# A new written order for the opening of a hybrid decoder step, with the state loads placed behind the gate's bias

## The chip, the cores and the metric

The kernel runs on one core of one Trainium2 chip. The metric is the device time of one execution in microseconds, lower is better; the kernel before took 1208.33 us, the median of three runs. The engines are TensorE (PE, matrix products; PEld is its weight load), VectorE (DVE), ScalarE (ACT), GpSimd (POOL) and SyncE (SP), which here only issues transfers. Each engine works through its own list of instructions in order and waits where an operand isn't ready.

## The reference

One layer of a hybrid decoder is computed for a prompt of 1024 rows and for 64 sample rows (8 sequences of 8), with model width 1024:

```python
mod = silu(c) @ w_ada + b_ada
shift, scale, gate = split(mod, 3)
h = rmsnorm(x, norm_g) * (1 + scale) + shift
u_pool, z_pool, z_ssm, xbc, dt_raw, g_raw = split(h @ w_in, SPLITS)
p = (pool_mix(u_pool, pool_buf) * silu(z_pool)) @ w_pool_out
xbc_c = silu(causal_conv(xbc, conv_buf, conv_w, conv_b))
y = SSD(xbc_c, softplus(dt_raw + dt_bias), -exp(a_log), ssm_state) + d_skip * xs
s = gated_rmsnorm(y, silu(z_ssm)) @ w_ssm_out
x = x + gate * ((sigmoid(g_pool) * p + sigmoid(g_ssm) * s) @ w_o)
```

`pool_buf` and `conv_buf` (the last rows of the pooling branch and of the convolution) and `ssm_state` are states that the sample rows bring along; new ones are returned beside the final rmsnorm of `x`.

## The kernel before

Everything is held transposed, 128 channels on the partitions and the 1088 rows (1024 of the prompt, 64 of the samples) along the free axis, in three blocks of 256, 384 and 448 rows (`BLK`). A product in full precision is made of three in a shorter format: each operand is cut into a high half (a copy in that format) and a low half (the rest, a subtraction), and high times high, low times high and high times low are summed.

The program has two parts. The **opening** (`first`, L604 on) reads `x`, normalizes and transposes it, forms the modulation from `w_ada`, makes `h` with both halves, and computes the first columns of `h @ w_in`: two of the gate's columns directly (L817), then a pair of columns by seven half-sized products (L958), `dt` (L843) and the `gate` vector (L870). Behind it the column pairs go on through `product` (L412), and then the rest of the layer. The order in the later part is found by a planner; the order of the opening is written by hand: the string `ORDER1` is a list of words, each word calls one short function that emits the instructions of one step, and `in_line` ties the instructions of each engine to each other in the order in which they were emitted. So the place of a word sets where its instructions stand on each engine that it uses. A letter behind a word names the engine: `.V` is DVE, `.G` POOL, `.A` ACT.

The words that this text speaks of (`b` a block, `k` one of eight slices of 128 channels):

- `warmN`: N matmuls whose result nobody reads. `sq`, `root`, `unit`, `spread`, `rsb`: the norm of the rows, spread over the partitions. `turn`b.k and `out`b.k: the transposed tile on PE, and its product with the norm on DVE (L703) into the tile `tf`.
- `ada`p.k: part p of silu(c) @ w_ada on PE (L736). `mr`, `end`, `md`: its copy, its transposition (L744) and the scale and shift, `md0` to `md3` for two slices each (L751, L754).
- `h`b.k: high half of `h` on ACT (L767, L769). `t`, `ta`: the same value in full in `tf` (L776 on ACT, L778 on DVE; for sample columns L785 and L786). `l`b.k: its low half (L644).
- `hi`, `lo`: halves of the first gate-column weights. `pr`b.k: six matmuls of block b with slice k (L817). `sg`: sigmoid and store.
- `ca`, `cb`, `cc`, `ce`: sums and differences of the halves of `tf` (L644, 544 columns) for the seven products; `s1h` to `s4h` and `s1l` to `s4l` their halves; `wh`, `wl` halves of the weight sums; `tc`, `tb`, `d21`, `d12` the weight sums. `m`i.s: twelve matmuls (L958). `u`i.s: their sums.
- `dU`, `dL`, `dR`: the matmuls of `dt` (L843), which read `tf` after the `c` words. `gt`, `ge`: the gate's matmuls (L870), and its sum with the bias on DVE followed by its store to `gate_d`.

`loads` runs after each word and issues, in the order of the list `waiting`, each transfer whose conditions have been said; they go to SP's queue. PSUM banks are handed out in the order of the words. Behind the opening `u_unit` and `conv_unit` begin with loads of the states into small tiles of four buffers; these loads are not part of the written order, and the planner sets them where it finds a place on SP. `tc.issue_after(i)` keeps an instruction behind instruction i on its engine's list.

Of the kernel before, what the change touches and what calls it, by code (L numbers as in the profile page):

```python
# [8 lines left out]
F32 = mybir.dt.float32  # L9
# [37 lines left out]
def tile_pool_ssd_step(  # L47
# [473 lines left out]
    yp_ = [None] * 4  # L521

    def u_unit(gi):
        L = gi + 1
        stp = sm.tile([P, 120], F32, tag="stc", name=nm("stp"), bufs=4)
        load(stp, state_pool[gi])
        pwt = sm.tile([P, P], F32, tag="stc", name=nm("pwt"), bufs=4)
        load(pwt, pool_w[0, gi])
# [66 lines left out]
    def gate_load(k):  # L595
# [21 lines left out]
        ta2.6.A wl4.V pr1.6 l1.7.V sgt t2.6 t2.7 m1.0 cb1.V sg0.0 cc1.V sg0.1 pr1.7 ce1.V h2.7 s1l0.V h2.6
        pr2.5 sg1.1 l2.7.V sg1.0 m1.1 l2.6.V d12.V s4h1 ca2.V pr2.6 wh5 cb2.V s1h2 ca3.V pr2.7 s1l2.V
        s1h3 cb3.V cc2.V gt0 wh3 u1.0 sg2.0 wl3.G u1.1 dR0 wh2 gt2 sg2.1 ce2.V dR1 cc3.V s2h0 gt4 wl2.V
        s4h2 dU1 ce3.V s2h3 s4l2.V s2h2 dL0 dUo1 s2l3.V dU0 s4h3 s2l0.V z1.0 s2l2.V gt6 dUo0 s1l3.V s2h1 dL1  # L620
        ge s4l1.G s3h0 dLo0 m2.0 s3h1 dLo1 s3h3 s3l1.V s3h2 s2l1.V m2.1 u2.0 dsL s3l3.V z1.1 s3l2.V m3.0
# [1668 lines left out]
```

## Time and profile before

| | before |
|---|---|
| median of 3 runs | 1208.33 us (1208.1 to 1209.11) |
| the profiled execution's own time | 1206.63 us |
| its span, first to last instruction | 1204.9 us |
| granted TensorE clock in the span | 0.998 |
| busy: PE, DVE, ACT, POOL | 99%, 76%, 55%, 68% |
| first L412 matmul, the end of the opening on PE | 90.43 us |

Times in the rows are microseconds from the start of the span, unless marked ns. In an order of time, a row is its start, its length, the engine, the line, the operation, the tiles it writes and reads, and a count where neighbours were merged; what stands in brackets is the idle time of the engine ahead of it and what ended it. Matmuls overlap, so that their starts tell more than their lengths.

### The profile page before, as it was taken

What the parts mean: (1) busy time and instruction counts of PE and PEld (TensorE: products, weight loads), DVE (VectorE), ACT (ScalarE), POOL (GpSimd) and SP (SyncE); (2) the same over time, 40 slices, a digit from 0 to 9 for tenths busy, and PEclk for the clock granted to TensorE, in tenths of its full rate; (3) what the DMA queues carried; (4) which work ended last, traced back from release to release, by engine and by line L of the source; (5) the groups of instructions that cost most, each with busy time, mean ns of one, the idle gap of its engine ahead of it and who ended that gap; (6) DMA issues with size and microseconds to landing.
All of it is one profiled execution on the core that took longest, in us unless ns stands there. A gap on an engine that the chain in (4) does not pass through costs nothing.

```text
span 1204.9 us, 25116 instructions
## 1 busy us (share of the span) xinstructions
PE 1190.0 (99%) x9274; PEld 1125.3 (93%) x9274; DVE 915.8 (76%) x1567; ACT 661.4 (55%) x1511; POOL 815.0 (68%) x687
## 2 busy tenths in 40 slices
PE   9999999999999999999999999999999999999997
PEld 8879999999999999999999999999999989999885
DVE  6993689975979587877576564687888988679976
ACT  6864356475665556554534334566686766412435
POOL 1127878877988787755677776376889889523653
PEclk9999999999999999999999999999999999999999
DMA  9836445565546555454576767988788788595794
GB/s 352 305 133 208 141 137 180 185 212 149 185 157 201 172 160 164 149 166 137 191 241 239 239 220 252 322 311 267 238 273 297 263 293 282 204 337 157 236 208 158
DMA packets 156082, 262.69 MB, mean 218 GB/s; under 512 B 31280, under 2 KB 79160, under 8 KB 155960
## 3 DMA queue, kind: packets, MB, share of 16 engines
q1 hardware_dynamic: 87208, 171.25, 42.7%
q10 hardware_dynamic: 64592, 81.91, 19.7%
q0 software_dynamic: 4160, 7.94, 3.1%
q8 instruction: 73, 1.20, 0.4%
q14 instruction: 49, 0.40, 0.1%
HBM read 173.31 MB, written 87.73 MB: 217 GB/s over the span
## 4 chain that ended last, share of the span: by engine, by line
PE 82%; DVE 5%; DMA 4%; POOL 3%; ACT 3%; issue 2%; SPq 0%; DVEq 0%; POOLq 0%; ACTq 0%
PE mm L412 24%; PE ps L412 24%; PE mm L227 15%; PE pc L412 5%; PE ps L1246 2%; PE ps L1249 2%; DMA Y<-in_w_ada 1%; PE ps L2043 1%; PE ps L2042 1%; PE ps L2041 1%; DVE tf L644 1%; PE ps L1513 1%; PE ps L958 1%; PE pc L1335 1%; DMA G<-in_w_ada 1%
## 5 line engine op out<-in xcount | busy, mean ns | idle before, releaser
L227 PE MATMUL mm<-Y,w 128*128 128x352 f32 (+1 forms) x1440 | 255.4, 331 | 0.8 <-DVE G L1976 0.6
L227 PEld LDWEIGHTS mm<-Y,w 128*128 128x128 f32 x1440 | 235.3, 188 | 7.6 <-issue 4.6
L154 POOL TENSOR_TENSOR w<-rawA,w 128x512 fp32r<-128x512 f32 x120 | 181.7, 1518 | 78.6 <-ACT w L151 72.2
L154 POOL TENSOR_TENSOR w<-raw,w 128x512 fp32r<-128x512 f32 x90 | 157.2, 1753 | 62.9 <-ACT w L151 62.7
L412 PE MATMUL mm<-Y,w 128*128 128x272 f32 x1200 | 168.7, 289 | 0.0
L412 PE MATMUL ps<-Y,w 128*128 128x272 f32 x1200 | 167.8, 289 | 0.0
L412 PEld LDWEIGHTS mm<-Y,w 128*128 128x128 f32 x1200 | 156.8, 188 | 2.6 <-issue 1.0
L412 PEld LDWEIGHTS ps<-Y,w 128*128 128x128 f32 x1200 | 157.1, 188 | 0.8 <-issue 0.6
L151 ACT ACTIVATE w<-rawA 128x512 fp32r<-128x512 f32 x120 | 75.2, 626 | 95.1 <-PE ps L412 53.8
L1090 DVE SCALAR_TENSOR_TENSOR GA<-GA,cvT,GA 128x1112 f32<-128x1112 f32 x72 | 126.1, 1756 | 0.1
L151 ACT ACTIVATE w<-raw 128x512 fp32r<-128x512 f32 x90 | 56.0, 628 | 102.7 <-PE ps L412 33.7
L412 PE MATMUL mm<-G,w 128*128 128x272 f32 x720 | 101.2, 289 | 0.0
L412 PE MATMUL ps<-G,w 128*128 128x272 f32 x720 | 100.6, 289 | 0.0
L412 PEld LDWEIGHTS mm<-G,w 128*128 128x128 f32 x720 | 94.1, 188 | 1.2 <-issue 0.9
L412 PEld LDWEIGHTS ps<-G,w 128*128 128x128 f32 x720 | 94.4, 188 | 0.3 <-issue 0.3
L1234 ACT ACTIVATE dec<-dec,acT 128x128 f32<-128x128 f32 x256 | 78.6, 390 | 18.7 <-POOL dec L1230 18.6
L291 POOL TENSOR_TENSOR pw<-pw 128x512 fp32r<-128x512 f32 x40 | 65.6, 1639 | 11.5 <-ACT pw L290 11.5
L412 PE MATMUL pc<-Y,w 128*128 128x272 f32 x480 | 67.2, 288 | 0.0
L412 PEld LDWEIGHTS pc<-Y,w 128*128 128x128 f32 x480 | 62.6, 188 | 0.5 <-issue 0.4
L1470 POOL TENSOR_TENSOR Y<-xb,Y 128x512 fp32r<-128x512 f32 x32 | 41.5, 1296 | 25.0 <-ACT Y L1468 24.8
L1246 PE MATMUL ps<-dec,xd 128*64 128x128 f32 (+1 forms) x576 | 52.3, 273 | 0.6 <-DVE dec L1535 0.5
L1527 POOL TENSOR_TENSOR xl<-xw,xh 128x512 fp32r<-128x512 f32 x32 | 42.5, 1327 | 14.6 <-ACT xh L1526 14.6
(542 smaller groups left out, 2712.0 us busy)
## 6 DMA issues: line engine op xcount, KB each, us to landing
rawA<-in_w_in SPq DMA_DIRECT2D x62, 512.0 KB
ws<-pw ACTq DMA_DIRECT2D x32, 512.0 KB
dec<-acs_d SPq DMA_DIRECT2D x32, 512.0 KB
w<-ws SPq DMA_DIRECT2D x32, 512.0 KB
xbc<-GA ACTq DMA_DIRECT2D x24, 512.0 KB
wo<-ph SPq DMA_DIRECT2D x20, 512.0 KB
Y<-wo SPq DMA_DIRECT2D x10, 1024.0 KB
pw<-in_w_ssm_out ACTq DMA_DIRECT2D x32, 256.0 KB
```

The lines of the kernel that those rows point to most:

```text
L151: ins = act(hi[:, :, :ncols], raw[:, :, :ncols], AF.Copy)
L154: (eng or nc.gpsimd).tensor_tensor(lo[:, :, :ncols], raw[:, :, :ncols], hi[:, :, :ncols].bitcast(F32), ALU.subtract)
L227: mm(ps[:, :n], w[k // 4][h][:, k % 4, :], r[k][:, o:o + n], start=(j == 0), stop=(j == len(terms) - 1))
L291: nc.gpsimd.tensor_tensor(raw.bitcast(F32R), raw, hi.bitcast(F32), ALU.subtract)
L412: mm(p, w[j // 8][:, k], A(k, s)[j // 4 == 1], start=(j == 0), stop=(j == 11))
L644: eng[e].tensor_tensor(dst, x, y, op)
L1090: V.scalar_tensor_tensor(d[:, :n], rp[:, k:k + n], cvT[:, 24 * k + mc:24 * k + mc + 1], d[:, :n], ALU.mult, ALU.add)
L1234: act(dec[:, h], dec[:, h], AF.Exp, bias=acT[:, c, 8 * g + h:8 * g + h + 1], scale=-1.0)
L1246: mm(o[hh], xd[:S, 2 * q + hh, :], dec[:S, 2 * q + hh], start=True, stop=state is None)
L1249: mm(o[hh], state[:, h * 64:h * 64 + 64], cE[:, h], start=False, stop=True)
L1470: nc.gpsimd.tensor_tensor(yl[g][:, :, o:o + S], v, yhc.bitcast(F32), ALU.subtract)
L1527: nc.gpsimd.tensor_tensor(xl, xw, xh.bitcast(F32), ALU.subtract)
```

## The change

`ORDER1` is written anew: nearly the same words in another order, 350 before and 349 now. The `warm` matmuls ahead of the first `turn` grow from 20 to 25, and those behind it shrink from 18 to 11. These words change engine: `lo0.0`, `l2.1`, `l1.3`, `l2.4`, `l1.4`, `wl3` and `s4l1` from POOL to DVE, `l0.5` from DVE to POOL, `ta2.1` and `t0.3` from ACT to DVE, `t0.2` and `t0.4` from DVE to ACT, `unit1` from DVE to ACT. The loads change: `vecs` goes behind the fifth tile of `x`, the first of the two first weight pieces ahead of the sample rows, the second behind part 0 of `w_ada`. The state loads of the first `u_unit` and `conv_unit` go behind the last load of the gate's bias. One tile of the sigmoid has a tag of its own (`g3`).

```diff
     def u_unit(gi):
         L = gi + 1
         stp = sm.tile([P, 120], F32, tag="stc", name=nm("stp"), bufs=4)
-        load(stp, state_pool[gi])
         pwt = sm.tile([P, P], F32, tag="stc", name=nm("pwt"), bufs=4)
-        load(pwt, pool_w[0, gi])
+        with tc.issue_after(calm[0]):
+            load(stp, state_pool[gi])
+            load(pwt, pool_w[0, gi])
...
     ORDER1 = """
-        warm20 sq0.A silu sq1.V turn0.3 turn0.5 turn0.2 tab vt sq2.V turn0.6 turn0.1 root0
...
+        warm20 sq0.A silu sq1.V warm5 turn0.0 turn0.2 turn0.3 warm2 sq2.V tab root0 sq3.A sq4.A
...
-                buf = pa.tile([P, HF], F32, tag=("u3", "u2", "c2", "u3")[2 * b + t], name=nm("g0"))
+                buf = pa.tile([P, HF], F32, tag=("u3", "u2", "c2", "g3")[2 * b + t], name=nm("g0"))
...
-                load(bg[32 * j:32 * j + NB + 1], b_ada[0, 2 * D + 256 * j:2 * D + 256 * j + 256].partition_broadcast(NB + 1))
+                ins = load(bg[32 * j:32 * j + NB + 1], b_ada[0, 2 * D + 256 * j:2 * D + 256 * j + 256].partition_broadcast(NB + 1))
+            calm.append(ins.ins)
...
-        for what in ("x01", "vb", "x27", "smp", "p0", "w", "p1", "p2"):
+        for what in ("x01", "x24", "vb", "x57", "w0", "smp", "p0", "w1", "p1", "p2"):
...
     def conv_unit(mc, g, row):
         stc = sm.tile([P, 24], F32, tag="stc", name=nm("stc"), bufs=4)
-        load(stc, state_conv[mc])
+        with tc.issue_after(calm[0]):
+            load(stc, state_conv[mc])
```

Behind the opening the lists of all engines are the same as before but for a few neighbours. Three places in the opening, as the built programs have them. The first is POOL from the end of its settings (`bg`) to the first weight half of the later part (L154). Before:

```order
L999 MEMSET bg 128x256
L644 TENSOR_TENSOR w_489<-raw_243,w_489 128x512
L644 TENSOR_TENSOR Y_520<-tf_310,Y_519 128x448
L644 TENSOR_TENSOR Y_520<-tf_290,Y_519 128x384
L644 TENSOR_TENSOR G_761<-tf_315,G_760 128x448
L644 TENSOR_TENSOR G_761<-tf_315,G_760 128x384
L644 TENSOR_TENSOR w_1057<-raw_931,w_1057 128x512
L644 TENSOR_TENSOR Y_520<-tf_294,Y_519 128x544
L644 TENSOR_TENSOR w_1213<-rawA_715,w_1213 128x512
L154 TENSOR_TENSOR w_1254<-rawA_1250,w_1254 128x512
```

Now:

```order
L1004 MEMSET bg 128x256
L649 TENSOR_TENSOR G_747<-tf_363,G_746 128x256
L649 TENSOR_TENSOR w_1207<-rawA_709,w_1207 128x512
L154 TENSOR_TENSOR w_1249<-rawA_1245,w_1249 128x512
L154 TENSOR_TENSOR w_1305<-rawA_1245,w_1305 128x512
```

Of eight low halves on POOL one is left (`wl6`, the last ahead of L154), and `l0.5` is new.

The second is DVE from the first product of the sample block (`out2.k`, 128x448; `raw`, `w` are `lo0.0`) to `md0` (the rows that write `md`). Before:

```order
L703 TENSOR_TENSOR tf_298<-ps_405,rsb 128x448
L703 TENSOR_TENSOR tf_366<-ps_423,rsb 128x448
L703 TENSOR_TENSOR tf_310<-ps_435,rsb 128x448
L703 TENSOR_TENSOR tf_315<-mm_412,rsb 128x448
L703 TENSOR_TENSOR tf_290<-ps_483,rsb 128x448
L751 TENSOR_TENSOR md<-ps_491,vT 128x18
```

Now:

```order
L708 TENSOR_TENSOR tf_345<-ps_436,rsb 128x448
L708 TENSOR_TENSOR tf_363<-ps_423,rsb 128x448
L708 TENSOR_TENSOR tf_345<-mm_414,rsb 128x384
L708 TENSOR_TENSOR tf_299<-ps_441,rsb 128x448
L708 TENSOR_TENSOR tf_349<-mm_400,rsb 128x384
L649 TENSOR_TENSOR w_446<-raw_237,w_446 128x512
L708 TENSOR_TENSOR tf_295<-ps_395,rsb 128x448
L756 TENSOR_TENSOR md<-ps_497,vT 128x18
```

Seven instructions stand there now where five stood.

The third is DVE at the last of the `c` words (`tf<-tf,tf`, 128x544; the `c` tile is `u1`, the `w` row `wl2`, `Y`, `S` and `R` low halves of sums), whose results the `dt` matmuls read. Before:

```order
L976 TENSOR_TENSOR c_125_1059<-s_110_900,ps_964 128x272
L976 TENSOR_TENSOR c_125_1059<-s_110_900,mm_1008 128x272
L644 TENSOR_TENSOR tf_306<-tf_306,tf_298 128x544
L644 TENSOR_TENSOR tf_290<-tf_366,tf_290 128x544
L644 TENSOR_TENSOR w_1071<-rawA_633,w_1071 128x512
L644 TENSOR_TENSOR tf_366<-tf_366,tf_290 128x544
L644 TENSOR_TENSOR Y_520<-tf_306,Y_519 128x544
```

Now:

```order
L649 TENSOR_TENSOR tf_349<-tf_349,tf_299 128x544
L649 TENSOR_TENSOR tf_303<-tf_358,tf_303 128x544
L981 TENSOR_TENSOR c_127_1086<-s_109_895,ps_994 128x272
L649 TENSOR_TENSOR tf_358<-tf_358,tf_303 128x544
L981 TENSOR_TENSOR c_127_1086<-s_109_895,ps_962 128x272
L649 TENSOR_TENSOR Y_1082<-tf_295,Y_1082 128x544
L649 TENSOR_TENSOR Y_1082<-tf_303,Y_1082 128x544
L649 TENSOR_TENSOR Y_1082<-tf_299,Y_1082 128x544
L649 TENSOR_TENSOR w_1063<-rawA_622,w_1063 128x512
```

The weight half and one of the two `u1` sums have moved behind the last `c` word (`tf_366` before, `tf_358` now).

More of the change, by code (lines that the diff above doesn't have):

```diff
@@ L617, in tile_pool_ssd_step @@
[L617 to L621, printed above, removed]
@@ L624, in tile_pool_ssd_step @@
+        s2l0.V s2h2 dL0 z1.0 s2h1 s2l3.V s2l2.V dL1 dUo1 wh3 wl2.V dUo0 s1l3.V s4l2.V
+        gt6 s3h0 wl3.V dLo1 s3h3 s4h3 m2.1 s3h1 dLo0 s2l1.V m2.0 s3l0.V s3h2 ge
+        z1.1 s3l1.V u2.0 m3.0 wh6 wl6.G s3l2.V u2.1 s3l3.V m3.1 dRo1 dRo0 u3.1 u3.0
+        s1l1.V m4.0 nw m4.1 dsR s4l1.V wl5.V u4.0 s4l0.V s4l3.V m5.0 nt3 m5.1 dsL
+        u5.0 u4.1 n1 nt2 m6.0 u5.1 n2 u6.0 z5.0 m6.1 z5.1 nd u6.1
     """.split()
@@ L1020, in first @@
                 waiting += [((), lambda: load(xr[8][0][:NS], x_sample.rearrange("b t d -> (b t) d")))]
[L1021 to L1022 removed]
+            elif what[0] == "w":
+                waiting += [((), lambda t=int(what[1]): w_load(t, 0))]
             elif what[0] == "x":
```

38 lines of the change are left out of this document (20 added, 18 removed).

## The prediction

> **What bounds the kernel now.** I read the busy time by stretches first, then TensorE's order of time in the opening, then VectorE's and GpSimd's. In the stretches the columns are the busy time of each engine with its instructions in brackets, the granted clock, the DMA share and GB/s.
>
> ```profile
> 92.00:300.00 208.00, 208.00 (x1643) 206.62 (x1643) 147.71 (x236) 112.01 (x256) 164.72 (x109) 1.00 0.54 173
> 300.00:600.00 300.00, 300.00 (x2374) 295.59 (x2373) 231.00 (x360) 170.82 (x384) 228.51 (x152) 1.00 0.53 170
> 600.00:900.00 300.00, 299.69 (x2440) 279.27 (x2441) 208.16 (x389) 165.25 (x398) 213.17 (x196) 1.00 0.76 259
> ```
>
> From 92 to 900 us TensorE (PE, the first busy figure) is without a gap: 807.69 of 808 us. The change touches nothing there, so what it gains or loses by the first L412 matmul should arrive at the end nearly whole. The question is when that matmul starts. PE's order of time in the opening (start, length, then the instruction, its count, and in brackets the idle time ahead):
>
> ```profile
> 29.65 0.28 PE L817 MATMUL ps<-Y,w 128*128 128x256 f32 x1
> ...
> 34.55 0.33 PE L817 MATMUL ps<-Y,w 128*128 128x384 f32 x1
> ...
> 35.41 0.34 PE L817 MATMUL mm<-Y,w 128*128 128x384 f32 x1
> 35.68 1.95 PE L736 MATMUL pc<-G,scT 128*32 128x128 f32 x64
> ...
> 39.48 0.28 PE L817 MATMUL mm<-Y,w 128*128 128x256 f32 x1
> ...
> 40.43 0.28 PE L817 MATMUL mm<-Y,w 128*128 128x256 f32 x1
> ...
> 41.80 1.96 PE L736 MATMUL pc<-G,scT 128*32 128x128 f32 x64
> ...
> 47.46 0.39 PE L817 MATMUL mm<-G,w 128*128 128x256 f32 x1 [0.18 <-DVE G L644]
> ...
> 52.58 1.78 PE L958 MATMUL ps<-Y,w 128*128 128x272 f32 x12 [0.30 <-ACT s L974]
> 54.20 0.28 PE L817 MATMUL mm<-G,w 128*128 128x256 f32 x1
> ...
> 60.38 0.36 PE L817 MATMUL ps<-G,w 128*128 128x448 f32 x1
> ...
> 61.38 0.36 PE L817 MATMUL mm<-G,w 128*128 128x448 f32 x1
> ...
> 65.60 1.07 PE L870 MATMUL pc<-Y,scT 128*32 128x256 f32 x16
> ...
> 71.25 0.42 PE L843 MATMUL ps<-tf,dwd 128*32 128x272 f32 x1 [0.84 <-DVE tf L644]
> ...
> 72.49 0.87 PE L843 MATMUL ps<-tf,dtw 128*32 128x272 f32 x9 [0.57 <-DVE tf L644]
> ...
> 75.31 1.75 PE L958 MATMUL mm<-G,w 128*128 128x272 f32 x12
> ...
> 78.40 3.18 PE L958 MATMUL ps<-Y,w 128*128 128x272 f32 x24
> 81.42 3.17 PE L958 MATMUL mm<-Y,w 128*128 128x272 f32 x24
> ...
> 90.43 1.68 PE L412 MATMUL ps<-Y,w 128*128 128x272 f32 x12
> ```
>
> A word of the written order is one call; `pr0.1` is six matmuls of block 0 (256 columns) with slice 1 of the rows. The row at 29.65 is its last, so it ends at about 29.77. From there to 90.43 are 60.66 us. How much of that is work follows from starts of neighbours: five steps from 34.55 to 35.41 are 0.172 us each, so a `pr` of 384 columns is 1.03; eight from 39.48 to 40.43 are 0.119, a `pr` of 256 is 0.71; five from 60.38 to 61.38 are 0.20, a `pr` of 448 is 1.20. The 24 of L958 from 78.40 to 81.42 are two `m` words, 1.51 each. An `ada` part (35.68, 41.80) takes 1.9.
>
> Work left behind `pr0.1`: six `pr` of 256 (4.26), eight of 384 (8.24), eight of 448 (9.60), two and a half `ada` parts (4.75), three short transposes (0.3, estimate), `gt` and `dt` from 65.60 to 75.31 without the two idle times (9.71 − 1.41 = 8.30), fourteen `m` (21.14). The sum is 56.6, so **TensorE loses 4.1 us** in this piece, of which 1.41 lie before L843 at 71 to 72 us, and 1.0 between 47.46 and 54.20 (6.74 us for two `m`, two 384 and one 256, 5.79). The remaining 1.7 are small waits. 4.1 us is the most that a better order behind `pr0.1` can bring.
>
> What PE waits for is named DVE (VectorE). DVE and GpSimd (POOL) there:
>
> ```profile
> 43.44 2.30 POOL L644 TENSOR_TENSOR G<-tf,G 128x448 fp32r<-128x448 f32 x2 [2.97 <-ACT G L769]
> ...
> 66.80 1.38 POOL L644 TENSOR_TENSOR w<-raw,w 128x512 fp32r<-128x512 f32 x1 [21.06 <-ACT w L802]
> 68.14 1.84 POOL L644 TENSOR_TENSOR Y<-tf,Y 128x544 fp32r<-128x544 f32 x1
> ```
> ```profile
> 43.47 1.40 DVE L644 TENSOR_TENSOR G<-tf,G 128x256 fp32r<-128x256 f32 x1
> 44.79 1.09 DVE L644 TENSOR_TENSOR dwd<-dtw 128x128 f32<-128x128 f32 x1
> ...
> 66.96 1.80 DVE L644 TENSOR_TENSOR tf<-tf,tf 128x544 f32<-128x544 f32 x1
> ...
> 69.38 1.19 DVE L644 TENSOR_TENSOR tf<-tf,tf 128x544 f32<-128x544 f32 x1
> ```
> ```profile
> L644 DVE TENSOR_TENSOR tf<-tf 128x544 f32<-128x544 f32 x4 | 2.9, 722 | 0.1
> L644 DVE TENSOR_TENSOR Y<-tf,Y 128x256 fp32r<-128x256 f32 x4 | 1.7, 418 | 0.2 <-ACT tf L776 0.2
> ```
>
> The last two rows are the group means (ns) of ordinary DVE subtractions: 0.418 us at 256 columns, 0.722 at 544. While POOL runs a subtraction of its own, DVE's take 1.40 and 1.80 instead.
>
> **The change part by part.** *Halves moved from POOL to DVE.* Seven low halves leave POOL (`lo0.0`, `l2.1`, `l1.3`, `l2.4`, `l1.4`, `wl3`, `s4l1`) and one small one goes there (`l0.5`). On a line between 0.418 and 0.722 they cost DVE 0.69 + 0.62 + 0.55 + 0.62 + 0.55 + 0.69 + 0.72 = 4.44 us; `l0.5` gives back 0.42. The other letters that change (`ta2.1` and `t0.3` to DVE, `t0.2`, `t0.4` and `unit1` to ACT) give about −0.6 by the same lengths. Against this 3.4 stands the stretching that ends: 0.98 (1.40 for 0.418) and at least 0.67 (1.09 for at most 0.42) at 43 to 46 us, 1.08 and 0.47 at 67 to 70.6, 3.2 us for four POOL subtractions. For the three others the bounds are nothing and the same share (2.4); I take 1.5. `l0.5` on POOL brings back up to 1.0. So DVE's load in the opening is 3.4 − 3.2 − 1.5 + 1.0, about −0.3 us: level, between −1.5 and +1.5. The gain is therefore not less work; it is where the work stands.
>
> [...]
>
> *The early part.* The sample rows are loaded behind 256 KB of weights more, and four 448-column products, two of 384 and `lo0.0` now stand on DVE between `rsb2` and `md0`, where five products of 448 stood:
>
> ```profile
> 22.24 1.69 DVE L703 TENSOR_TENSOR tf<-ps,rsb 128x448 f32<-128x448 f32 x3 [1.84 <-ACT rsb L691]
> ...
> 24.91 0.17 DVE L751 TENSOR_TENSOR md<-ps,vT 128x18 f32<-128x18 f32 x1
> 25.11 0.67 DVE L754 TENSOR_TENSOR md<-md,vT 128x18 f32<-128x18 f32 x1
> ```
> ```profile
> 25.91 1.20 ACT L767 ACTIVATE Y<-tf,md 128x384 fp32r<-128x384 f32 x2 [1.00 <-DVE md L751]
> ...
> 28.27 2.40 ACT L776 ACTIVATE tf<-tf,md 128x256 f32<-128x256 f32 x4
> ```
>
> Before: 2.67 us for five, 0.53 each. After: 4 × 0.53 + 2 × 0.47 + 0.65 = 3.7, so +1.0, and 0.4 for the load (0.66 at most, 256 KB at 398 GB/s, from the stretch 26 to 33 us below). L754's 0.67 stood beside POOL's `lo0.0`; without it some 0.2, as the L751 row beside it, −0.5. So DVE comes to `md0` at 26.3 instead of 24.91 and has it ready near 26.8, 0.9 later than the 25.9 at which ACT began before. Then ACT did a 384-column `h1.0` ahead of `h0.0`, and `t0.1`, the first of the four at 28.27 (0.60 each), ended at 28.9; now `h0.0`, `h0.1`, `t0.0`, `t0.1` come straight behind `md0`, four times 0.5 (0.60 less overlap), to 28.8. `pr0.1` therefore ends at 29.7 to 29.8 in both: price 0, bounds −0.5 to +0.9.
>
> *The middle.* Behind it DVE's line is shorter at three places. The first is `md1`: no waiting for ACT's `t0.x`, and POOL's `l2.1` no longer beside it. The second is 43 to 46 us, without the 1.65. The third is the `c` words that make the operands of L843. The last of them, `ce3`, let PE go at 72.49. Ahead of it no longer stand `wl2` (0.69), one 272-column sum (0.42 at most) and the stretching by two POOL subtractions (1.55); with about 1 us of lead from the first two places (estimate, bounds 0 and 2) it ends near 68.8. TensorE has 39.4 us of work between `pr0.1` and `dL0` (all `pr` and `ada` 26.85, four `m` 6.0, three `gt` at 1.05, six of the eight `dt` calls at 0.51, the transposes), so it can't be there before 69.1, and by my sum is at 70. So the 1.41 go. `u0.0` on ACT stands now behind one copy of `s1`, where it stood behind `t0.6` and two copies, so most of the 1.0 around `m0.1` goes (0.8). Of the 1.7 in small waits I take half, 0.85. New waits: `l0.6` is ready some 0.2 us before `pr0.6` needs it and `wl5` 0.5 before `m5.0`; POOL's `wl6` runs beside DVE there. I set 0.2 for these, bounds 0 and 1.5. Sum: 1.41 + 0.8 + 0.85 − 0.2 = **2.9 us earlier**, L412 at about 87.5.
>
> *The loads.* The state loads leave their place between the first weights and `w_ada`'s last part:
>
> ```profile
> 26.04 0.33 SPq L526 DMA_DIRECT2D stp<-in_state_pool x1
> ...
> 31.20 0.33 SPq L798 DMA_DIRECT2D raw<-in_w_in x1
> ```
> ```profile
> 26.00:33.00 7.00, 7.00 (x89) 6.00 (x82) 5.82 (x16) 6.89 (x13) 0.56 (x1) 1.00 1.04 398
> 33.00:39.00 6.00, 5.87 (x85) 4.96 (x84) 5.32 (x15) 4.54 (x10) 0.65 (x2) 1.00 0.93 324
> ```
>
> Four issues take SP from 26.04 to 31.20, and then the stream falls from 398 to 324 GB/s. Six microseconds at that rate miss 0.44 MB, 1.1 us, and what is queued behind (the last `w_ada` part, the dt weights, two columns, the gate weights) lands 1 to 2 us earlier now. But PE's rows at 41.80 and 65.60, which read the first and the last of them, carry no wait. Price 0. It could cost something only if the four loads held up the first column pair, and that is issued behind `ge`, after the last L870 matmul; their own first readers stand behind the opening.
>
> The profiled execution took 1206.63 us with a span of 1204.9; its span would become 1202.0, its time 1203.7. The median of the runs, 1208.33, lies 1.7 above the profiled time, so I forecast 1208.3 − 2.9 = **1205.4 us**.
>
> **The rivals.** *Half of it* (1206.9): the words are so tight that each lost wait returns elsewhere. For it: the estimated leads of 0.2 to 0.8 us before `pr0.6`, `dU1`, `m3` and `m5`; if DVE runs 1 us later than I add up, those return 1.5 us. Against it: PE's idle is now in few large pieces, which a lead of 1 us covers.
>
> *Nothing arrives* (1208.3): the first column pair sets L412. Its loads stand behind `gate_d`, behind `ge`; the price is that L412 can't move more than `ge` does. Against it: `ge` needs only the gate matmuls, which stand before 75.31, so 15 us lie between it and L412. Part of it is the case that the early part's +0.9 is not regained.
>
> *Slower* (1210.5): DVE is the bound, and the stretching was not POOL's doing. Then the 3.4 us of moved work are added whole, with 0.9 at `md0`; DVE's reserve is 1.9 us (1.18 idle in 26 to 33, 0.68 in 33 to 39), so L412 comes 2.4 us less what is left of small waits, 2.2 us, later. It decides if the DVE rows of 256 columns still take 1.4 us around 43.
>
> **How the numbers follow.** Forecast 0.55, half of it 0.28, nothing 0.09, slower 0.08. The measurement can tell about 0.2% (2.4 us) from no change. The forecast's own range is a gain of 2.4 to 4.7, so 1203.6 to 1205.9; with half of it and part of no change the range is 1203.2 to 1208.6 us. Faster by over 0.2% has 0.56 (the forecast and a little of the next), within it 0.36, slower 0.08.
>
> **What would show it.** The first L412 row at 87 to 88 us. No idle brackets before L843. DVE's 256- and 544-column subtractions at 0.42 and 0.72 throughout 24 to 75 us. `md` for the first time at 26.3, later than before. GB/s near 400 from 33 to 39 us, with PE none the wiser. Wrong it is if L412 starts after 89.5, if DVE is still stretched, or if L412 starts early and a PE gap behind 92 us takes the gain back.

## The result and the profile after

The changed kernel takes 1202.99 us, the median of 6 runs (1201.98 to 1205.44), against 1208.41 us of the kernel before (6 runs beside it, 1207.87 to 1209.8). The ratio is 0.9956, with an interval of 0.9944 to 0.9969: 5.4 us faster. The forecast was 1205.4 us, 2.9 us faster, with a range down to 1203.2. The direction was right, and the size was little more than half of what came.

Line numbers of the changed kernel are up to seven higher: L644 is now L649, L736 L741, L786 L791, L817 L822, L843 L848, L870 L875, L958 L963. TensorE's order of time in the changed kernel, from the end of `pr0.1` to the first L412 matmul:

```profile
28.26 0.28 PE L822 MATMUL ps<-Y,w 128*128 128x256 f32 x1
28.47 1.08 PE L741 MATMUL pc<-G,scT 128*32 128x128 f32 x32
...
34.29 1.95 PE L741 MATMUL pc<-G,scT 128*32 128x128 f32 x64
...
39.99 1.95 PE L741 MATMUL pc<-G,scT 128*32 128x128 f32 x64
...
47.35 1.68 PE L963 MATMUL ps<-Y,w 128*128 128x272 f32 x12
...
50.94 1.68 PE L963 MATMUL ps<-Y,w 128*128 128x272 f32 x12
...
62.70 2.80 PE L875 MATMUL pc<-Y,scT 128*32 128x256 f32 x48
...
68.07 1.10 PE L848 MATMUL ps<-tf,dtw 128*32 128x272 f32 x16
...
85.07 1.68 PE L412 MATMUL ps<-Y,w 128*128 128x272 f32 x12
```

No row in this stretch has a bracket: TensorE waits for nothing. The first L412 matmul is at 85.07 instead of 90.43 us. The half part of `ada` that follows `pr0.1` starts at 28.47 instead of 29.86, so 1.39 us are won ahead of it, and from it to L412 are 56.60 us instead of 60.57, so 3.97 behind it. The prediction had counted 56.6 us of work there: all of the loss is gone, not 2.9 us of it.

The stretches behind the opening, which the prediction held to pass the gain on:

```profile
92.00:300.00 208.00, 208.00 (x1643) 206.62 (x1642) 154.02 (x240) 113.71 (x259) 164.59 (x109) 1.00 0.56 176
300.00:600.00 300.00, 300.00 (x2374) 295.60 (x2373) 231.22 (x360) 170.47 (x380) 228.84 (x153) 1.00 0.53 169
600.00:900.00 300.00, 299.75 (x2438) 279.20 (x2437) 211.36 (x389) 166.42 (x403) 215.39 (x199) 1.00 0.78 260
```

From 92 to 900 us TensorE is without a gap (807.75 of 808 us), as before. Behind 900 us the executions of one and the same kernel differ. The profiled execution of the changed kernel was the longest of its six (1205.44, span 1203.7), that of the kernel before took 1206.63, so this pair alone would show 1.2 us. Here is the longest wait of TensorE behind 900 us in that execution, and then the same wait in another one of the same kernel (a row says who waits for whom, then the total in us, the number of times and the longest):

```profile
PE ps L1253 <- DVE cE L1544: 2.9, 1, 2.9
```
```profile
PE ps L1253 <- DVE cE L1544: 0.2, 1, 0.2
```

The same wait costs 2.9 us in the one, 0.2 in the other (span 1199.6) and 1.5 in a third. So a median of few totals can be off by about 1 us (an estimate from these three), and **the start of the first L412 matmul is the better measure of the opening**; I use it below beside the medians. Three profiled executions of each kernel give 90.43, 91.26 and 90.81 before (mean 90.83) and 85.07, 86.13 and 85.03 after (mean 85.41): 5.42 us, as much as the medians differ.

### The profile page after: what moved, and what is told of

Read it like the earlier page. It is cut to its first block, busy times and chain, and to the rows that moved or that the text cites. A ratio compares the mean times of both kernels' runs of the same rounds, so it can differ in the third digit from the quotient of the medians.

```text
span 1203.7 us, 25096 instructions
## 1 busy us (share of the span) xinstructions
PE 1188.0 (99%) x9270; PEld 1125.3 (93%) x9270; DVE 919.7 (76%) x1570; ACT 662.6 (55%) x1514; POOL 806.9 (67%) x681
## 4 chain that ended last, share of the span: by engine, by line
PE 78%; POOL 5%; DVE 5%; issue 5%; DMA 3%; ACT 2%; SPq 0%; POOLq 0%; DVEq 0%; ACTq 0%
PE mm L412 24%; PE ps L412 23%; PE mm L227 12%; PE pc L412 5%; PE ps L1253 2%; PE ps L1256 1%; PE ps L963 1%; PE ps L822 1%; PE mm L822 1%; DVE G L1989 1%; DMA dec<-acs_d 1%; POOL Y L1477 1%; ACT dec L1241 1%; DMA R<-in_w_o 1%; POOL ph L1787 1%
## 5 line engine op out<-in xcount | busy, mean ns | idle before, releaser
L154 POOL TENSOR_TENSOR w<-rawA,w 128x512 fp32r<-128x512 f32 x120 | 182.0, 1521 | 78.3 <-ACT w L151 74.0
L154 POOL TENSOR_TENSOR w<-raw,w 128x512 fp32r<-128x512 f32 x90 | 157.4, 1755 | 62.7 <-ACT w L151 62.4
L412 PE MATMUL mm<-Y,w 128*128 128x272 f32 x1200 | 168.7, 289 | 0.0
L412 PE MATMUL ps<-Y,w 128*128 128x272 f32 x1200 | 167.8, 289 | 0.0
L412 PEld LDWEIGHTS mm<-Y,w 128*128 128x128 f32 x1200 | 156.8, 188 | 2.6 <-ACT w L151 0.8
L412 PEld LDWEIGHTS ps<-Y,w 128*128 128x128 f32 x1200 | 157.1, 188 | 0.8 <-issue 0.6
L412 PE MATMUL mm<-G,w 128*128 128x272 f32 x720 | 101.2, 289 | 0.0
L412 PE MATMUL ps<-G,w 128*128 128x272 f32 x720 | 100.6, 289 | 0.0
L412 PEld LDWEIGHTS mm<-G,w 128*128 128x128 f32 x720 | 94.0, 188 | 1.2 <-issue 0.9
L412 PEld LDWEIGHTS ps<-G,w 128*128 128x128 f32 x720 | 94.4, 188 | 0.3 <-issue 0.3
L412 PE MATMUL pc<-Y,w 128*128 128x272 f32 x480 | 67.2, 288 | 0.0
L412 PEld LDWEIGHTS pc<-Y,w 128*128 128x128 f32 x480 | 62.6, 188 | 0.5 <-issue 0.4
```

What stands on the lines that cost most here:

```text
L154: (eng or nc.gpsimd).tensor_tensor(lo[:, :, :ncols], raw[:, :, :ncols], hi[:, :, :ncols].bitcast(F32), ALU.subtract)
L412: mm(p, w[j // 8][:, k], A(k, s)[j // 4 == 1], start=(j == 0), stop=(j == 11))
```

## The experiments

One table first. "Front" is the start of the half `ada` part that follows `pr0.1`, "between" the time from there to the first L412 matmul (both from TensorE's order of time), "third tile" the start of VectorE's square of it, "rows" the start of ACT's square of the sample rows. Times are in us. Ratios are to the kernel before, run beside it on the same chip; its own median moved from 1208.2 to 1209.3 between the groups of runs, so medians of different rows are not to be compared to the tenth.

| program | third tile | rows | front | between | L412 | median (runs), ratio |
|---|---|---|---|---|---|---|
| before | 8.23 | 17.34 | 29.86 | 60.57 | 90.43 | 1208.41 (6) |
| before, second profile | 8.58 | 18.25 | 30.76 | 60.50 | 91.26 | 1207.89 (1) |
| before, third profile | 8.48 | 17.45 | 29.97 | 60.84 | 90.81 | 1209.35 (1) |
| changed | 7.17 | 16.32 | 28.47 | 56.60 | 85.07 | 1202.99 (6), 0.9956 [0.9944, 0.9969] |
| changed, second profile | 8.01 | 17.34 | 29.52 | 56.61 | 86.13 | 1202.95 (4), 0.9949 [0.9935, 0.9962] |
| changed, third profile | 7.22 | 16.34 | 28.49 | 56.54 | 85.03 | 1201.29 (1) |
| before + order | 8.36 | 17.56 | 29.71 | 57.69 | 87.40 | 1204.05 (7), 0.9967 [0.9956, 0.9977] |
| before + loads and states | 9.94 (behind `vt`) | 17.11 | 29.56 | 60.39 | 89.95 | 1206.84 (11), 0.9987 [0.9978, 0.9996] |
| before + letters | 8.32 | 17.58 | 30.20 | 59.31 | 89.51 | 1206.96 (11), 0.9984 [0.9975, 0.9993] |
| before + tile | 7.89 | 17.23 | 29.87 | 60.07 | 89.94 | 1208.18 (10), 0.9994 [0.9985, 1.0003] |
| before + order + tile | 8.79 | 17.78 | 30.57 | 56.61 | 87.18 | 1205.49 (7), 0.9973 [0.996, 0.9985] |
| changed, eight letters back | 7.22 | 16.29 | 28.64 | 57.61 | 86.25 | 1203.45 (5), 0.9957 [0.9944, 0.9969] |
| changed, these back but `s4l1` | 7.14 | 16.15 | 28.46 | 56.57 | 85.03 | 1201.75 (4), 0.9949 [0.9934, 0.9964] |
| changed, states back | 8.07 | 17.43 | 29.55 | 57.49 | 87.04 | 1203.86 (4), 0.9945 [0.9927, 0.9963] |
| changed, tile shared | 7.13 | 16.13 | 29.33 | 58.14 | 87.47 | 1205.08 (5), 0.9957 [0.9943, 0.9972] |
| changed, `vecs` early | 8.18 | 18.25 | 31.16 | 56.61 | 87.77 | 1205.04 (5), 0.9966 [0.9952, 0.998] |
| changed, rows first | 7.14 | 15.67 | 28.69 | 56.61 | 85.30 | 1201.61 (4), 0.9932 [0.9918, 0.9947] |
| changed, less filler | 7.16 | 15.55 | 28.19 | 56.60 | 84.79 | 1201.64 (5), 0.9948 [0.9935, 0.9962] |

The column "between" lies at 56.54 to 56.61 in all eight profiles in which TensorE doesn't wait there, while "front" moves by up to 1.1 us from one execution of a kernel to the next. Differences in "between" are therefore of the program; of the front, only means and repeated differences are. The totals are too coarse for single parts: order with tile (0.9973) can't be told from order alone (0.9967), and no ratio of the five kernels with a part taken back lies outside the interval of the changed kernel. What is said of parts below rests on TensorE's rows, mostly of one profile each.

### Order, loads, letters: each part alone on the kernel before

The new written order with all its letters, nothing else (the five letters beside the eight low halves were never tried apart, so they count with the order here):

```diff
     ORDER1 = """
-        warm20 sq0.A silu sq1.V turn0.3 turn0.5 turn0.2 tab vt sq2.V ...
+        warm20 sq0.A silu sq1.V warm5 turn0.0 turn0.2 turn0.3 warm2 sq2.V ...
```

> The kernel before with the new written order (its letters included) and nothing else: the loads, the states and the sigmoid's tag stay. Theory (the gain is 1.3 us up to pr0.1, from the new place of vecs among the loads, plus 4.1 us behind it, from the written order): the sample rows still land at about 17.3 us, md0 is ready at 25.9 or later, pr0.1 ends near 29.8, and behind it TensorE has at most 0.3 us of waits, so the first L412 matmul is at 86.3 to 86.8 us and the median about 1204.4. Rival (the loads bring the middle's gain, because the weights arrive sooner): L412 at 89 or later, 1207. A second rival, that the new order needs the new loads: PE waits for weights (DMA as releaser) and L412 is at or behind 90.4.

L412 came at 87.40, behind the theory's 86.3 to 86.8. "Between" fell by 2.9 us, from 60.64 (the mean of before) to 57.69, and the front, 29.71, is within 0.2 us of before's earliest. The gain behind `pr0.1` is of the order, not of the loads, as expected; but "between" stayed 1.1 us above 56.6. What kept it there stands on ACT (first this run, then the changed kernel):

```profile
61.90 0.49 ACT L833 ACTIVATE g<-mm 128x384 f32<-128x384 f32 x1 [1.90 <-DMA gs<-g]
```
```profile
59.09 0.49 ACT L835 ACTIVATE g<-mm 128x384 f32<-128x384 f32 x1 [0.40 <-ACT g L835]
```

The fourth half tile of the sigmoid (`sg1.1`) shares a buffer with the first (`sg0.0`), whose store to memory is still under way; ACT stands for 1.9 us until that store is done. The tile's own tag `g3` takes this away. The prediction had not priced that edit at all.

The new loads and the states' place, with the old order (`x` are the tiles of `x`, `vb` is `vecs`, `w` the first weight pieces, `smp` the sample rows, `p` the parts of `w_ada`):

```diff
-        for what in ("x01", "vb", "x27", "smp", "p0", "w", "p1", "p2"):
+        for what in ("x01", "x24", "vb", "x57", "w0", "smp", "p0", "w1", "p1", "p2"):
...
+        with tc.issue_after(calm[0]):
+            load(stp, state_pool[gi])
+            load(pwt, pool_w[0, gi])
```

> The kernel before with the new load order and the state loads behind the gate's bias, and the old written order and letters. Theory: the third tile of x no longer comes 1.2 us late, the sample rows land at 16.3 instead of 17.3, md0 is ready 1.0 us sooner, but the old order's waits of 4.1 us behind pr0.1 stay: L412 at 89.1 to 89.6 us, median about 1207.2. Rival (the loads carry most of it): L412 at 87 or earlier, 1205 or less. If the old order can't use it (PE waits behind DVE as before from the same point): L412 at 90.4, 1208.4.

L412 at 89.95, later than the theory's 89.6: the old order can hardly use the earlier rows. VectorE shows why, and then ACT:

```profile
9.86 0.17 DVE L715 TENSOR_SCALAR vT<-vT 128x8 f32<-128x8 f32 x1 [2.72 <-DMA vT<-in_vecs]
9.94 1.22 DVE L659 SCALAR_TENSOR_TENSOR sqj<-Y 128x1024 f32<-128x1024 f32 x1
```
```profile
15.68 0.49 ACT L693 ACTIVATE rsb<-ps 128x384 f32<-128x384 f32 x1 [2.21 <-PE ps L684]
...
17.11 1.04 ACT L661 ACTIVATE sqj<-R 64x1024 f32<-64x1024 f32 x1
```

In the old order the word `vt`, which reads `vecs`, stands ahead of the square of the third tile. With `vecs` loaded later VectorE stands for 2.72 us at `vt`, and that square starts at 9.94 (8.23 before), where the theory had it sooner. What follows is late too: ACT waits 2.21 us for the second tile group's sums, and the rows' square has no bracket, so the rows are there and ACT comes to them late. The new order has `vt` behind the squares of the first five tiles; the new loads need that order.

The letters of the eight low halves alone:

```diff
-  ... lo0.0.G ... l2.1.G ... l1.3.G ... l2.4.G ... l1.4.G ... wl3.G ... s4l1.G ... l0.5.V
+  ... lo0.0.V ... l2.1.V ... l1.3.V ... l2.4.V ... l1.4.V ... wl3.V ... s4l1.V ... l0.5.G
```

> The kernel before with only the engine letters of eight low halves changed: lo0.0, l2.1, l1.3, l2.4, l1.4, wl3 and s4l1 on DVE instead of POOL, l0.5 on POOL instead of DVE; order and loads stay. Theory (DVE's load stays level since POOL's subtractions no longer stretch it; the gain is where the work stands): DVE rows of 256 columns near 43 us take 0.42, and L412 comes at 89.4 to 90.9, the median 1207.3 to 1208.8. Rival (the stretching by POOL is most of the 4.1 us): L412 at 87.5 or earlier, 1205.5 or less. Other rival (the 4.4 us moved to DVE are added whole): L412 at 92 or later, 1210.

L412 at 89.51 and "between" 1.3 us shorter than before's 60.64. DVE's load stayed level: it is busy for 77.08 of the first 92 us, against 77.15 before. Groups of DVE's sums and subtractions in the opening (count, busy us, mean ns), before and with the letters moved:

```profile
L644 DVE TENSOR_TENSOR tf<-tf,tf 128x544 f32<-128x544 f32 x12 | 10.0, 849 | 0.1
L644 DVE TENSOR_TENSOR G<-tf,G 128x256 fp32r<-128x256 f32 x4 | 2.7, 663 | 0.0
```
```profile
L644 DVE TENSOR_TENSOR tf<-tf,tf 128x544 f32<-128x544 f32 x12 | 8.5, 720 | 0.2
L644 DVE TENSOR_TENSOR G<-tf,G 128x256 fp32r<-128x256 f32 x3 | 1.3, 418 | 0.0
```

The stretching is POOL's doing: 849 ns fall to 720, 663 to 418. That refutes the rival in which the 4.4 us of moved work are added whole.

The sigmoid's own tile alone:

```diff
-                buf = pa.tile([P, HF], F32, tag=("u3", "u2", "c2", "u3")[2 * b + t], name=nm("g0"))
+                buf = pa.tile([P, HF], F32, tag=("u3", "u2", "c2", "g3")[2 * b + t], name=nm("g0"))
```

> The kernel before with only the sigmoid's fourth tile in a buffer of its own. Theory (the old order's waits before L843 are DVE's and ACT's lines of work, to which the 1.0 us that ACT stood before that tile adds a part): ACT's wait for the store is gone, the two waits before L843 shrink from 1.4 to 0.4 to 1.1 us, L412 at 89.5 to 90.4, median 1207.6 to 1208.6. Rival (this one wait was most of the old loss): both waits gone, L412 at 89.0 or earlier.

ACT's wait is gone (that tile's sigmoid starts at 60.98 instead of 62.08), the two waits before L843 fall from 1.4 to 1.1 us, "between" by 0.5 us. The old order is mostly not held by this tile.

Order and tile together:

> The kernel before with the new written order and the sigmoid's own tile, loads and states at their old places. Theory (order and tile together take all of the old 4 us behind pr0.1, and the loads act ahead of it): between pr0.1 and the first L412 matmul 56.6 us, at most 57.5 if the last w_ada part is late as it was with the states alone put back; pr0.1 at 29.5 to 30.3 as before, L412 at 86.1 to 87.6. Rival (the tile cost 1.5 us only beside the new loads): more than 57.5 behind pr0.1, with waits behind DVE or ACT.

```profile
30.57 1.08 PE L739 MATMUL pc<-G,scT 128*32 128x128 f32 x32
...
87.18 1.68 PE L412 MATMUL ps<-Y,w 128*128 128x272 f32 x12
```

56.61 us between, without a wait, on the old loads. So **order and tile make the whole gain behind `pr0.1`**, 4.1 us of means (60.64 to 56.58), and loads and states have no part in it. The front, 30.57, is as late as before: most of that part needs the loads.

### One part of the change taken back

All eight letters back:

> The changed kernel with the letters of the same eight low halves put back (seven on POOL, l0.5 on DVE); order and loads are the new ones. Theory (letters and order belong together: POOL's subtractions take 1.2 to 1.8 us each against 0.4 to 0.7 on DVE and stretch DVE beside them): L412 at 85.8 to 87.5 us, with waits of 0.7 to 2.4 us on TensorE behind DVE or POOL, the median 1203.7 to 1205.5. Rival (the order alone does it): L412 at 85.0 to 85.4 and no wait, 1203.0.

L412 at 86.25, within the theory's range, but with one wait and not many. TensorE, and POOL's rows there:

```profile
83.76 1.14 PE L963 MATMUL mm<-Y,w 128*128 128x272 f32 x7 [0.76 <-POOL Y L649]
```
```profile
80.55 1.41 POOL L154 TENSOR_TENSOR w<-rawA,w 128x512 fp32r<-128x512 f32 x1 [2.65 <-ACT w L151]
81.91 1.80 POOL L649 TENSOR_TENSOR Y<-tf,Y 128x544 fp32r<-128x544 f32 x1
```

`s4l1` stands on POOL behind a weight piece of the main loop, which itself waited 2.65 us for ACT, and takes 1.80 us; `m6.0` waits for it. Next, all of the eight letters back but that one:

> The changed kernel with six low halves back on POOL and l0.5 on DVE, only s4l1 stays on DVE. Theory (the run with all letters back lost its 1.0 us at the one wait for POOL's s4l1, and POOL's stretching of DVE lies in DVE's slack): 56.6 us from pr0.1 to L412 and no wait on TensorE, L412 at 85.0 to 86.2, median 1202.9. Rival (DVE stretched by POOL loses it in small pieces): 57.0 or more, waits behind DVE.

```profile
L649 DVE TENSOR_TENSOR G<-tf,G 128x256 fp32r<-128x256 f32 x4 | 2.5, 656 | 0.0
```
```profile
28.46 1.08 PE L741 MATMUL pc<-G,scT 128*32 128x128 f32 x32
85.03 1.68 PE L412 MATMUL ps<-Y,w 128*128 128x272 f32 x12
```

DVE is stretched again (656 ns, and busy for 76.9 of the first 92 us against 75.6), and TensorE doesn't notice: 56.57 us. In the new order six of the seven moves from POOL to DVE bring nothing; the stretching lies in DVE's slack. Only `s4l1` is worth its move, 1.0 us.

The tile shared again:

> The changed kernel with the sigmoid's fourth tile back in the buffer it shared (u3 instead of g3). Theory (the tile's own buffer is what lets ACT go on; the new order with the shared one showed ACT waiting 1.9 us for the store of the tile before): ACT waits 1.5 to 2 us for that store near 60 us, DVE's c words come 0.3 to 0.5 later, TensorE waits 0.5 to 1.2 us at m2 and behind, L412 at 85.9 to 86.4, median 1203.8 to 1204.4. Rival (that second microsecond of the order-only run came from its late loads): L412 at 85.0 to 85.4.

"Between" is 58.14 us: the tile is worth 1.5 us in the changed kernel (1.1 with the old loads, 57.69 to 56.61). ACT waits 2.27 us for the store, VectorE's last `c` words follow (0.7 us later than in the changed kernel, counted from the front), and TensorE shows it at the `m` words (ACT first, then TensorE):

```profile
61.83 0.49 ACT L835 ACTIVATE g<-mm 128x384 f32<-128x384 f32 x1 [2.27 <-DMA gs<-g]
```

```profile
73.40 1.75 PE L963 MATMUL mm<-G,w 128*128 128x272 f32 x12 [0.50 <-ACT tf L861]
...
75.98 4.15 PE L963 MATMUL ps<-Y,w 128*128 128x272 f32 x31 [0.20 <-DVE Y L649]
```

L412 was later than the theory's 86.4 mostly because this execution's front was 0.9 us late; why, stands in the last section.

The states loaded at their old place:

> The changed kernel with the four state loads back at their old place (issued between the weights and the last part of w_ada); all else as changed. Theory (price 0: the last w_ada part and the gate weights arrive in time either way): GB/s in 33 to 39 us falls from about 404 to about 325, the first L412 matmul stays at 85.0 to 85.4 us, no wait on TensorE, median 1203. Rival (with the new order, which reaches ada2 1.4 us sooner, the weights set the pace): TensorE waits for a DMA at ada3 or at the gate product, L412 at 86 to 87, 1204 to 1205.

The theory (price 0) fell, and the rival came: TensorE waits for a transfer, L412 is at 87.04. TensorE, and the stretch from 33 to 39 us:

```profile
43.25 0.64 PE L740 MATMUL pc<-G,scT 128*32 128x128 f32 x16 [0.66 <-DMA G<-in_w_ada]
```
```profile
33.00:39.00 6.00, 6.00 (x89) 5.40 (x89) 5.71 (x18) 5.27 (x10) 0.00 (x0) 1.00 0.82 246
```

The stream falls to 246 GB/s, and the last quarter of `w_ada`'s last part is 0.66 us late; "between" grows by 0.9 us. With the old loads the same place cost nothing in order and tile (56.61), where the stream fell only to 330 GB/s and TensorE came to that part at 42.09. It came at 41.80 in the trace of before and did not wait, at 41.81 in before + tile and waited 0.17 us, and at 41.07 here. So the old place was already near to costing something, and a front that comes forward makes it cost; the changed kernel comes to that part at 39.99. One profile stands behind the 0.9 us, and why the stream falls lower here than with the old loads is not shown.

`vecs` early again:

```diff
-        for what in ("x01", "x24", "vb", "x57", "w0", "smp", "p0", "w1", "p1", "p2"):
+        for what in ("x01", "vb", "x24", "x57", "w0", "smp", "p0", "w1", "p1", "p2"):
```

> The changed kernel with vecs back behind the second tile of x, all else as changed. Theory (vecs among the first tiles makes the third tile's last piece land 1.2 us late, and the engines that are late stay so up to the sample rows): the third tile at 8.2 instead of 7.1, ACT's square of the sample rows at 17.3 to 17.9 instead of 16.3, md0 1.0 to 1.6 later, L412 at 86.1 to 86.7, no new wait behind pr0.1, median 1204 to 1204.7. Rival (a load of 22 KB can't matter, the order of words made the front faster): L412 at 85.0 to 85.4.

The third tile's square is at 8.18, the rows' at 18.25, L412 at 87.77, all of it ahead of `pr0.1` ("between" 56.61); rows and L412 came later than the theory had them. Here is TensorE's wait for the rows:

```profile
18.30 0.45 PE L703 MATMUL ps<-ident,R 128*128 128x128 f32 x1 [1.94 <-DMA R<-in_x_sample]
```

In all eight profiles with `vecs` behind the second tile the third tile's square starts at 7.89 to 8.79. With `vecs` behind the fifth tile and the new order it starts at 7.13 to 7.22 in seven of nine, and near 8.0 in two. Both kernels were profiled twice more to see this:

> The kernel before once more, for the spread of its opening. Theory (vecs behind the second tile of x makes the third tile late every time): DVE's square of the third tile at 8.1 to 8.4 us, L412 at 90.0 to 91.2, with the same two waits before L843. If the lateness is chance: the square at 7.1 to 7.3 and L412 near 89.4.

> The changed kernel once more. Theory (the front depends on two things that differ from one execution to the next: when TensorE's filler matmuls pass from about 6.6 a microsecond to 11.5, and the sample rows; behind pr0.1 there is no wait in any execution): the first transpose at 8.2 to 9.4 us, pr0.1 28.4 to 29.6, L412 exactly 56.6 behind it, so 85.0 to 86.2; median 1202.5 to 1203.8. If the first profile was luck behind pr0.1 too: more than 56.9 between them, with a wait on TensorE.

> The kernel before a third time, for the front's spread. Theory (its third tile of x is always late): DVE's square of it at 7.9 to 8.6 us, pr0.1 at 29.8 to 30.8, 60.5 us from there to L412.

> The changed kernel a third time, for the front's spread. Theory (its third tile is late only now and then): the square at 7.1 to 7.2 us, or near 8.0 with one late piece; pr0.1 at 28.4 to 29.6, and 56.6 us from there to L412.

The mean front is 30.20 before and 28.83 after: 1.4 us. Of these 1.0 is the rows' (17.68 to 16.67 in the mean). The rest is the order's: from the rows' square to the front it takes 12.51 or 12.52 us in all three profiles of before, 12.15 to 12.18 in the three of the changed kernel, and 12.15 with the order alone (in other profiles, where TensorE or a tile of `x` is later than the rows, up to 13.20). The second profile of the changed kernel is one of the two late ones (8.01, rows 17.34), and its front is a microsecond behind the others. So the front's gain is of the change on the average, but not in every execution.

### Can more be had

The first weight piece, which the change puts ahead of the sample rows, behind them again:

```diff
-        for what in ("x01", "x24", "vb", "x57", "w0", "smp", "p0", "w1", "p1", "p2"):
+        for what in ("x01", "x24", "vb", "x57", "smp", "w0", "p0", "w1", "p1", "p2"):
```

> The changed kernel with the first weight piece (256 KB) behind the sample rows instead of ahead of them. Theory (behind md0 nothing waits, so whatever moves the sample rows moves L412): the rows' square on ACT at 15.6 to 15.8 instead of 16.3, md0 0.4 to 0.6 sooner unless part 0 of w_ada holds ada0, L412 at 84.5 to 84.9, median 1202.4. Rival (TensorE's transposes or the w_ada parts set md0): L412 at 85.0 to 85.2, 1203. Other rival (the first weight piece is late for hi0.0 and pr0.0): L412 behind 85.4.

The rows came 0.65 us sooner and L412 not at all (85.30): the first rival was nearer, TensorE sets the front in this execution. Its first transpose was at 8.80 us, behind the filler, where the changed kernel's first profile had it at 8.22. So the next version has less filler, and both weight pieces behind part 0 of `w_ada`:

```diff
-        warm20 sq0.A silu sq1.V warm5 turn0.0 ...
+        warm14 sq0.A silu sq1.V warm5 turn0.0 ...
...
-        for what in ("x01", "x24", "vb", "x57", "w0", "smp", "p0", "w1", "p1", "p2"):
+        for what in ("x01", "x24", "vb", "x57", "smp", "p0", "w0", "w1", "p1", "p2"):
```

> The changed kernel with the sample rows and part 0 of w_ada ahead of both first weight pieces, and 14 filler words instead of 20 at the start. Theory (the rows-first run gained nothing because TensorE, held by filler until 8.8 us, had become the later one, and part 0 lands just in time): the first transpose at 7.0 to 8.3 us, the rows' square at 15.5 to 15.8, md0 at 24.2 or sooner, L412 at 84.2 to 84.9, median 1201.0 to 1202.2. Rival (with less filler TensorE reaches its higher rate later and loses it again): first transpose no earlier than 8.2, L412 at 85 or later. Other rival (the first weights, now behind part 0, hold hi0.0 and pr0.0): a wait of TensorE behind md0, L412 at 85.2 or later.

First transpose at 7.58, rows at 15.55, L412 at 84.79, as the theory had it. That is 0.24 us before the earliest of three profiles of the changed kernel and 0.6 before their mean. Its median, 1201.64, and its ratio, 0.9948 [0.9935, 0.9962], can't be told from the changed kernel's, and no more can those of the version with the rows first (0.9932 [0.9918, 0.9947]). Both beat the kernel before; whether they beat the changed one stays open.

## Why the prediction was right and wrong

**What bounds the kernel** was right. TensorE is gapless from 92 to 900 us (807.75 of 808), and what L412 gained came out at the end (5.42 us in means of L412, 5.4 in medians).

**The work behind `pr0.1`**, 56.6 us, was right to the tenth, and so was the most that could be won there, 4.1 us. The step that failed is the sum under "The middle", 2.9 us. It granted 0.8 of the 1.0 around `m0.1`, half of the small waits, and took off 0.2 for new ones. Measured are 4.1: every wait went, no new one came. So half of the small waits was the wrong size: with all inputs ready early enough they went together.

**The early part**, "price 0, bounds −0.5 to +0.9", failed worst. The change brings 1.4 us there. The sum had the rows 0.4 us later, by the 256 KB ahead of them. They came 1.0 us sooner in two of three profiles, since `vecs` no longer delays the tiles (`vecs` early again: 18.25). The 256 KB do cost (0.65 us, the rows first), but less than `vecs` had cost. First the third tile and the rows before, then after:

```profile
8.23 1.22 DVE L657 SCALAR_TENSOR_TENSOR sqj<-Y 128x1024 f32<-128x1024 f32 x1 [0.95 <-DMA Y<-in_x_prompt]
...
17.34 1.06 ACT L659 ACTIVATE sqj<-R 64x1024 f32<-64x1024 f32 x1 [1.30 <-DMA R<-in_x_sample]
```
```profile
7.17 1.23 DVE L662 SCALAR_TENSOR_TENSOR sqj<-Y 128x1024 f32<-128x1024 f32 x1
...
16.32 1.06 ACT L664 ACTIVATE sqj<-R 64x1024 f32<-64x1024 f32 x1 [1.40 <-DMA R<-in_x_sample]
...
20.62 1.16 DVE L708 TENSOR_TENSOR tf<-ps,rsb 128x448 f32<-128x448 f32 x2 [1.04 <-ACT rsb L696]
...
24.44 0.18 DVE L756 TENSOR_TENSOR md<-ps,vT 128x18 f32<-128x18 f32 x1
...
24.95 1.09 ACT L772 ACTIVATE Y<-tf,md 128x256 fp32r<-128x256 f32 x2 [0.88 <-DVE md L756]
```

`md0` is used at 24.95, not after 26.8. The sum's other terms came as computed: VectorE's seven instructions ahead of `md0` took 3.82 us (20.62 to 24.44; 3.7 forecast), and from there ACT began after 0.5 us instead of 1.0. What it took as unchanged was not: from the rows' square to VectorE's first product of 448 columns are 4.30 us (16.32 to 20.62) instead of 4.90 (17.34 to 22.24). The row at 8.23 of before named the transfer as what VectorE waited for; the prediction read past it to the bytes in the queue. The two failed steps add up to the miss: 2.9 forecast, 1.2 more in the middle and 1.4 here make 5.5, and 5.42 were measured.

**Halves from POOL to DVE.** That the load stays level was right (these letters alone: 77.15 to 77.08 us of busy time). That POOL's subtractions stretch DVE's was right too (a mean of 849 ns for 544 columns with these halves on POOL, 720 without), but not that the new order needs the stretching gone. In the old order the move is worth 1.3 us of "between". In the new one it matters for `s4l1` alone, and there since POOL comes to it late, not by the stretching. With six halves on POOL again VectorE was stretched (656 ns for 420), and TensorE lost nothing of the 4.1 us (56.57 between).

**The state loads**, price 0, were right for the old front (56.61 us with them) and wrong for the new one (0.9 us, in one profile). The rows at 41.80 and 65.60 had no wait, but how near they were to one was not asked.

**The sigmoid's tile** was left out of the sum; it is worth 1.1 to 1.5 us in the new order and 0.5 in the old. A row of before showed the wait, had it been looked up:

```profile
62.08 0.49 ACT L830 ACTIVATE g<-mm 128x384 f32<-128x384 f32 x1 [1.02 <-DMA gs<-g]
```

**The rivals.** Half of it, nothing, and slower did not come. The DVE row of 256 columns near 43 us took 0.43 and not 1.4, which was the mark set for "slower". Of the marks, no brackets before L843 and near 400 GB/s from 33 to 39 us (405 measured) held, and so did VectorE's subtractions of 256 and 544 columns (means of 420 and 720 to 722 ns; a row of 448 beside `l0.5` still took 1.09 us); L412 at 87 to 88 and `md` "later than before" did not. There was no rival on the side of more gain, and so the range ended 0.2 us above the result.

## What to carry to other kernels

Where an engine without gaps follows a stage with waits, count the work of the stage: the difference is what a better order can win (4.1 us here), and an order that gets all inputs ahead can win all of it, as here, and not a share. Price every edit of a change, also a tile's tag: here a buffer whose last content was still being stored held its next writer up for 1.0 to 2.3 us. A transfer's price is not its bytes (22 KB ahead of the third tile had its square at 8.18 us instead of 7.17, 256 KB ahead of the rows cost them 0.65): look at who waits for the transfers around it, and when a stage moves forward, ask again of each load that was just in time.

## What the runs showed of the hardware

**A load of 22 KB that costs a microsecond.** `vecs` is 128 rows of 176 bytes. Behind the second tile it takes the stream down for a moment (5 to 6 us, kernel before, then the changed one; the last figure is GB/s):

```profile
5.00:6.00 1.00, 1.00 (x7) 1.00 (x6) 0.04 (x1) 0.99 (x4) 0.00 (x0) 1.00 1.00 326
```
```profile
5.00:6.00 1.00, 1.00 (x12) 1.00 (x11) 0.04 (x1) 0.99 (x4) 0.00 (x0) 1.00 1.01 410
```

The dip is there in all eight profiles with `vecs` behind the second tile (232 to 326 GB/s) and in none of the other ten (381 to 410). The microsecond behind it is low too (381 against 422 in these two). Together they miss 125 GB/s for 1 us, 0.13 MB, 0.3 us of the stream, and yet the next tile's square starts 1.1 us later. Why the last piece lags so far is not settled; the two late executions without `vecs` there say that it is not the only cause.

**Ahead of the sample rows' landing the stream falls.** Here it is in the changed kernel:

```profile
14.00:15.00 1.00, 0.95 (x7) 0.70 (x8) 1.00 (x3) 0.92 (x2) 0.00 (x0) 1.00 0.98 201
15.00:16.00 1.00, 0.40 (x4) 0.17 (x2) 1.00 (x3) 0.00 (x0) 0.00 (x0) 1.00 1.00 262
16.00:17.00 1.00, 0.63 (x6) 0.64 (x6) 1.00 (x3) 0.69 (x1) 0.00 (x0) 1.00 1.03 414
```

That is 201 and 262 GB/s beside 414. In both kernels the dip lies just ahead of ACT's square of the rows, which waits for their transfer: from 14 to 16 us in the changed one (square at 16.32), from 13 to 17 in the kernel before (274, 229, 242 and 336 GB/s, square at 17.34). What takes the stream down there is not shown.

**TensorE speeds up at a time that differs between executions.** The filler matmuls at the start run at 6 to 7 records a microsecond and then at 11 to 12. Windows of 1 us with TensorE's records in brackets, the changed kernel, and then the run with the shared tile:

```profile
4.00:5.00 1.00, 1.00 (x10) 1.00 (x10) 1.00 1.03 416
5.00:6.00 1.00, 1.00 (x12) 1.00 (x11) 1.00 1.01 410
```
```profile
5.00:6.00 1.00, 1.00 (x7) 1.00 (x6) 1.00 1.00 401
6.00:7.00 1.00, 1.00 (x8) 1.00 (x8) 1.00 1.05 426
7.00:8.00 1.00, 1.00 (x12) 1.00 (x11) 1.00 1.03 422
```

The step lies between 4 and 7 us in 18 profiles, though TensorE is busy without a gap from 2 us up to the step in each (from 1.07 in those that were read from the start), and the granted clock reads 1.00 throughout. Since the filler is a fixed number of matmuls, the first transpose moved with it, from 8.17 to 9.44 us in the eleven profiles with 25 filler words ahead of it. The 9.44 is the run with the shared tile: its rows came at 16.13, as early as any behind the weight piece, and yet its front was late. What sets the moment of the step is not shown.
